# A gated-delta chain in two parts: its recurrence beside the inverse of the next head, each part with its own stretch of the waits

## The chip, the cores and the metric

The kernel runs on one core of a Trainium2 chip. The core has a matrix engine (TensorE, "PE" in the profile, its weight loads "PEld"), a vector engine (VectorE, "DVE"), a scalar engine (ScalarE, "ACT"), a general engine (GpSimd, "POOL") and a queue engine (SyncE, "SP") that issues the DMAs here. Each engine works through its own list of instructions in order and waits for the others by semaphores. Matrix products land in PSUM, which has eight banks; everything else lies in SBUF. The metric is the device time of one execution in microseconds, lower is better.

## The reference

One decoder layer with two groups of heads that read the same normalised stream (2048 prompt rows, 16 meta rows, 8 samples of 4 rows; width 1024): four retention heads and four gated-delta heads of 128 columns, then an output projection, a normalisation and a SwiGLU feed-forward part. What matters here is the gated-delta head, computed in chunks of 128 rows:

```python
decay = jnp.exp(jnp.where(incl, G[..., :, None] - G[..., None, :], -jnp.inf))
lower = jnp.where(strict, kk * decay, 0.0) * beta[..., :, None]
a_mat = jnp.eye(C, dtype=q.dtype) + lower
sol = lax.linalg.triangular_solve(a_mat, rhs, left_side=True, lower=True, unit_diagonal=True)
w_v, w_k = sol[..., :D], sol[..., D:]
attn = jnp.einsum('bnhid,bnhjd->bnhij', q, k) * decay
...
def step(s, xs):
    wv, wk, at, qg, kt, cd = xs
    u = wv - jnp.einsum('bhcd,bhde->bhce', wk, s)
    o = jnp.einsum('bhcd,bhde->bhce', qg, s) + jnp.einsum('bhij,bhje->bhie', at, u)
    s = cd[..., None, None] * s + jnp.einsum('bhcd,bhce->bhde', kt, u)
    return s, o
...
o_g = (rms_norm(o_g) * gdn_norm_w.astype(f32)).reshape(bsz, L, W) * jax.nn.silu(gz.astype(f32))
```

So a head has two parts. The triangular system of each chunk depends on that chunk alone, so all chunks of a block are inverted together. The recurrence over the state `s` goes chunk by chunk, and a head's recurrence in one block follows its recurrence in the block before.

## The kernel before

The program is written out in full by Python. It has three stages: attention (both groups of heads), the output projection with its normalisation, and the feed-forward part. The change touches attention alone.

Attention runs over four blocks of 512 prompt rows, that is four chunks of 128; the first block also carries one short tile with the meta and sample rows, which has a chain of its own beside the main one (`side` in `gdn_chain`). In each block the eight heads follow each other in the order r0 g0 r1 g1 r2 g2 r3 g3, in the fourth block r0 g0 g1 r1 g2 g3 r2 r3, with r for retention and g for gated delta. Each head has two kinds of work.

The *projection* (`ret_proj`, `gdn_proj`) multiplies the block with the head's weights, in many matmuls into PSUM tiles `pj`: 128x256 for a retention head, 128x512 for a gated-delta head. Weights and activations are split in a high and a low part, three matmuls for each product. Both are generators that yield every few matmuls with the microseconds that these are reckoned to take: 20.5 us for a whole projection of a block without the short tile. The vector and scalar engines work on what a projection leaves: rotation for r, convolution and gates for g. The convolved q goes into tile `post0`, the gate into `zg`, two buffers each.

The *chain* (`ret_chain`, `gdn_chain` with `gdn_group`) is a long line of small steps, each on what the step before left, through PE and DVE or ACT in turn. It starts when the head's projection is over, and its steps are strewn among the matmuls of the projections that follow. These are the steps of a gated-delta chain by their lines in the profile:

- L878 decay exponents (from `mg`), L895 transposes of v, L892 and L900 the scaled keys `kp` and their transposes, L906 the product of the keys, L908 `LT`, its masked parts L917 (`Z`), L918 (`U`) on DVE and L920 (`Lm`) on POOL;
- L924 the first transpose, then six levels of the inverse: L930, then L932 on DVE, then L937 and L939, then two copies on ACT;
- L950 the residual, L951 and L953 on DVE; two refinements L958, each followed by L960 on DVE, which leaves `V`; L965 the attention matrix;
- the recurrence, for each of four chunks: L992 and L993 the products of the state with keys and queries, L995 `r` on DVE, L1000 its product with the inverse, L1001 `u` on ACT, L1009 with L1010 the state update `S_gdn`, L1011 with L1012 the output row;
- the output: a reciprocal root in about a dozen short DVE operations (L261 to L273), L1019 and L1021 the scaling, L1023 the transposes, L1027 the product with the gate into `Uf`, L1029 the store.

The chain is a generator too. After each step it yields a number out of `LAT`, the microseconds that its result is reckoned to take, and yields `None` between the inverse and the recurrence; before the change `gdn_chain` swallows that `None` and lets the rest of the short tile's chain go first there. `attn_block` calls `advance` at each yield of a projection:

```python
self.active[key] = [chain, 0.0]
...
c[1] -= us
while c[1] <= 0:
    w = next(c[0], None)
    ...
    c[1] += w * SLACK[key]
```

So one `r` and one `g` chain are active at a time, and a `g` chain waits 1.8 times the reckoned latency at each step. `start` first calls `finish`, which lets an unfinished chain run out with no projection in between.

The tile framework then puts the recorded instructions in an order for each engine: it moves an instruction ahead of another on its engine where its operands are reckoned to be there earlier and its buffer is free. Small products of the chain share three PSUM banks (`w`), the state products one (`sc`), the projections two (`pj`). `LT`, `mg`, `Uf`, `V0` and `V1` have one buffer each; `E`, `kT`, `vb` and `kp` have two. Before the change the output lies in the buffer of `V0`, and the gated output in that of `Uf`, both of which the next head's inverse writes.

Of the kernel before, what the change touches and what calls it, by code (L numbers as in the profile page):

```python
# [31 lines left out]
RMS_EPS = 1e-6  # L32
NBLK = 4
CPB = 4
SLACK = {"r": 1.0, "g": 1.8}
LN_AT = [(x, i) for x in ("r1", "g1", "r2", "g2") for i in (18, 26)]
LAT = [1.0, 0.7, 0.7, 0.7, 2.0, 0.7, 0.5, 1.2, 1.8, 0.9, 1.0, 1.0, 1.7, 1.0, 0.6, 0.5, 0.5]
LEVELS = (1, 2, 4, 8, 16, 32, 64)


# [196 lines left out]
class Builder:  # L237
# [599 lines left out]
    def gdn_chain(self, b, h, cvz, G, mixd):  # L837

        cv, zg, sk, kps = cvz
        tiles = self.tiles_of(b)  # L840
        t = 1 if b == 0 else 0
        main = self.gdn_group(b, h, cv, zg, sk, kps[-1], G, mixd, list(range(t, t + CPB)), tiles)
        side = self.gdn_group(b, h, cv, zg, sk, kps[0], G, mixd, [0], tiles) if b == 0 else iter(())
        for w in main:
            if w is None:
                yield from side
                continue
            yield w
            w = next(side, None)
            if w is not None:  # L850
                yield w
        if b == NBLK - 1:
            self.nc.sync.dma_start(out=self.O["gdn_p"][h], in_=self.S["gdn", h])

    def gdn_group(self, b, h, cv, zg, sk, kp, G, mixd, ts, tiles):
# [10 lines left out]
        big = lambda tag, bufs=1, dt=F32, n=None: mp.tile([128, m, n or (R if sp else 128)], dt, tag=pre + tag, name=tag, bufs=1 if sp else bufs)  # L866
# [103 lines left out]
        yield None  # L970
        S = self.S["gdn", h]
        ss = self.sm.tile([128, m], F32, tag="gss", name="gss")
        O = big("V0", n=128)
        orow = NS if sp else 128
        for i in range(m):
            c0 = col(i)
# [42 lines left out]
        nc.vector.tensor_tensor(out=rs, in0=rs, in1=cq[:orow], op=ALU.mult)  # L1019
        p = self.psc.tile([128, 4, 128], F32, tag="sc", name="sc")[:, :m, :orow]  # L1020
        nc.vector.tensor_tensor(out=O[:orow], in0=O[:orow], in1=rs.unsqueeze(2).broadcast_to([orow, m, 128]), op=ALU.mult)  # L1021
        for i in range(m):
            nc.tensor.transpose(p[:, i, :], O[:orow, i, :], self.ident[:orow, :orow])  # L1023
        c0 = col(0)
        mx = big("Uf")[:, :, :orow]
        z = zg[:, c0:c0 + m * orow].rearrange("p (a b) -> p a b", a=m)
        nc.vector.scalar_tensor_tensor(out=mx, in0=p, scalar=self.gwh, in1=z, op0=ALU.mult, op1=ALU.mult)  # L1027
        cm = c0 if sp or b else c0 - NMETA
# [35 lines left out]

    def advance(self, us):
        for key in list(self.active):
            c = self.active[key]
            c[1] -= us
            while c[1] <= 0:
                w = next(c[0], None)  # L1070
                if w is None:
                    del self.active[key]
                    break
                c[1] += w * SLACK[key]

    def start(self, key, chain):
        self.finish(key)
        self.active[key] = [chain, 0.0]

    def finish(self, key):  # L1080
        while key in self.active:
# [2 lines left out]
    def attn_block(self, b):  # L1084
        nc = self.nc
        mixd = self.mixd[b]
        tiles = self.tiles_of(b)
        n = len(tiles)
        xT = self.xp.tile([128, 2, 8, 560], F32R, tag="xT", name="xT")
        self.xT = xT[:, 0], xT[:, 1]  # L1090
        before = self.first_block() if b == 0 else self.turned(b)
        next(before)
        rt = self.gp.tile([128, 5, 192], F32, tag="rott", name="rott", bufs=1)
        self.rot = {ch: rt[:, t] for t, (rows, c0, ch) in enumerate(tiles)}
        if b == 0:
            nc.sync.dma_start(out=rt[:SP, 0], in_=self.I["rot"][0:SP, :])
        o = SP + 512 * b
        nc.sync.dma_start(out=rt[:, n - CPB:n], in_=self.I["rot"][o:o + 512, :].rearrange("(c p) n -> p c n", p=128))
        gates = self.gp.tile([128, 5, 8], F32, tag="gates", name="gates")[:, :n]
        if b == 0:  # L1100
            nc.vector.memset(gates, 0.0)
        G = {}
        gg = self.gdn_gates(b, gates, G)
        ln = self.phase_ln(b + 1) if b < NBLK - 1 else iter(())
        for x in self.order(b):
            h = int(x[1])
            got = []
            if x[0] == "r":
                self.finish("r")
                fill = self.ret_proj(b, h, gates, got, before if h == 0 else None)  # L1110
            else:
                fill = self.gdn_proj(b, h, G, got)
            for i, us in enumerate(fill):
                self.advance(us)
                self.age += 1
                if self.pend and self.age >= 3 and self.age % 2:
                    self.split(*self.pend.pop(0))
                if x == "g0" and i == 8:
                    next(gg, None)
                if (x, i) in LN_AT:  # L1120
                    next(ln, None)
            if x == "r0":
                next(gg)
            if x[0] == "r":
                self.start("r", self.ret_chain(b, h, got, mixd))
            else:
                self.start("g", self.gdn_chain(b, h, got, G, mixd))
        for _ in ln:
            pass

# [329 lines left out]
```

## Time and profile before

| | |
|---|---|
| median of three runs | 3085.02 us (3084.47 to 3089.49) |
| profiled execution: time, span | 3085.82 us, 3084.0 us |
| mean granted TensorE clock | 0.972 |
| instructions in the span | 47091 |
| DMA | 384.75 MB, 125 GB/s mean |

The profile gives busy time by engine, busy time in stretches of the span, who waited for whom, and the instructions in order of time. PE's busy time overlaps from one matmul to the next, since matmuls are pipelined: what a matmul costs the engine is read from one start to the next. The projections can be told from the chains by name: `pj<-wh,xT` and `pj<-wl,xT` belong to a retention head, `pj<-xT,wh` and `pj<-xT,wl` to a gated-delta head. In a row of the waits stand the instruction that waited, what ended the wait, the total, the number of waits and the longest.

### The profile page before, as it was taken

The numbers are of one execution on the slowest core, as the hardware profiler recorded it, in microseconds if no ns is written. First come the engines' busy times: TensorE is split into PE (matmuls) and PEld (weight loads), VectorE is DVE, ScalarE is ACT, GpSimd is POOL, SyncE is SP. The second block draws the span as 40 slices with busy tenths as digits, with TensorE's granted clock in tenths as the row PEclk, the third lists the DMA queues.
The fourth block names the chain that finished last, engine by engine and source line by source line (L and its number), as shares of the span: only waits on it lengthen the run. The fifth ranks groups of instructions, "written<-read, shape, count | busy, mean of one in ns | idle before, by whom it ended". The sixth has DMA issues, their size and how long they took to land.

```text
span 3084.0 us, 47091 instructions
## 1 busy us (share of the span) xinstructions
PE 2889.0 (94%) x17930; PEld 2564.3 (83%) x17930; DVE 2189.5 (71%) x4547; ACT 1139.4 (37%) x2571; POOL 1055.6 (34%) x927
## 2 busy tenths in 40 slices
PE   6999998999999999999959999989999999999995
PEld 6888887888888877887848888889999988999994
DVE  7778676666676676567767777896666689666667
ACT  2444433444443433432233333433333343333331
POOL 1332222221222122225644545354334335333332
PEclk8999998999999999999979999989999999999998
DMA  7544533443344323346652222432212243221211
GB/s 268 211 158 175 178 141 132 155 156 145 130 153 169 116 91 122 117 151 208 206 175 97 95 85 89 144 122 76 75 55 76 73 130 130 75 76 55 76 62 41
DMA packets 132275, 384.75 MB, mean 125 GB/s; under 512 B 18145, under 2 KB 53521, under 8 KB 115665
## 3 DMA queue, kind: packets, MB, share of 16 engines
q1 hardware_dynamic: 132048, 381.74, 35.5%
q8 instruction: 141, 2.31, 0.3%
q14 instruction: 86, 0.70, 0.1%
HBM read 294.14 MB, written 87.56 MB: 124 GB/s over the span
## 4 chain that ended last, share of the span: by engine, by line
PE 58%; DVE 22%; POOL 7%; issue 7%; ACT 4%; DMA 3%; SPq 0%; POOLq 0%; ACTq 0%; DVEq 0%
PE pj L366 17%; PE d L366 15%; POOL S L1264 4%; PE Y L366 4%; PE X L366 4%; PE Z L366 4%; PE W L366 2%; DVE dl L316 2%; DVE s34l L316 1%; ACT s34h L309 1%; DVE rqt L267 1%; POOL Lm L920 1%; DVE cacc L820 1%; DVE y L1356 1%; DVE lnst L284 1%
## 5 line engine op out<-in xcount | busy, mean ns | idle before, releaser
L366 PE MATMUL pj<-wh,xT 128*128 128x256 f32 (+2 forms) x2176 | 453.4, 296 | 9.1 <-ACT wh L309 3.7
L366 PE MATMUL pj<-xT,wh 128*128 128x512 f32 (+1 forms) x1280 | 378.2, 379 | 0.8 <-DVE kp L775 0.6
L366 PEld LDWEIGHTS pj<-wh,xT 128*128 128x128 f32 (+1 forms) x2176 | 354.4, 191 | 14.1 <-ACT wh L309 4.0
L366 PE MATMUL pj<-wl,xT 128*128 128x256 f32 (+3 forms) x1088 | 315.3, 290 | 0.5 <-POOL wl L316 0.5
L366 PE MATMUL d<-dl,fh 128*128 128x512 f32 (+1 forms) x748 | 299.9, 401 | 8.4 <-DVE dl L316 7.8
L366 PE MATMUL d<-dh,fh 128*128 128x512 f32 (+1 forms) x748 | 293.8, 393 | 6.6 <-DVE y L1356 6.5
L366 PE MATMUL d<-dh,fl 128*128 128x512 f32 (+1 forms) x748 | 297.2, 397 | 0.7 <-POOL fl L316 0.7
L316 POOL TENSOR_TENSOR fl<-ta,fh 128x384 fp32r<-128x384 f32 (+1 forms) x66 | 70.8, 1073 | 642.5 <-ACT fh L309 642.5
L1264 POOL TENSOR_TENSOR S<-fr 128x512 f32<-128x512 f32 x132 | 209.7, 1606 | 168.1 <-DVE s34l L316 108.6
L1356 DVE TENSOR_TENSOR y<-y,d 128x512 f32<-128x512 f32 (+1 forms) x352 | 238.9, 680 | 31.7 <-PE d L366 31.6
L366 PE MATMUL pj<-xT,wl 128*128 128x512 f32 (+1 forms) x640 | 228.9, 358 | 0.0
L366 PEld LDWEIGHTS pj<-xT,wh 128*128 128x128 f32 x1280 | 207.4, 191 | 19.6 <-DVE S L674 3.0
L366 PEld LDWEIGHTS pj<-wl,xT 128*128 128x128 f32 (+1 forms) x1088 | 207.6, 191 | 1.1 <-POOL wl L316 0.8
L366 PEld LDWEIGHTS d<-dl,fh 128*128 128x128 f32 (+1 forms) x748 | 137.9, 184 | 39.9 <-DVE dl L316 21.8
L366 PEld LDWEIGHTS d<-dh,fl 128*128 128x128 f32 (+1 forms) x748 | 137.9, 184 | 33.9 <-POOL fl L316 1.1
L316 DVE TENSOR_TENSOR a11l<-fr,a11h 128x512 fp32r<-128x512 f32 x66 | 52.1, 789 | 160.2 <-ACT a11h L309 160.2
L366 PEld LDWEIGHTS d<-dh,fh 128*128 128x128 f32 (+1 forms) x748 | 138.1, 185 | 29.4 <-DVE y L1356 9.8
L920 POOL TENSOR_TENSOR Lm<-LT,lvl 128x512 f16<-128x512 f32 (+1 forms) x108 | 138.4, 1315 | 35.0 <-DVE LT L908 28.5
L309 ACT CAST a11h<-fr 128x512 fp32r<-128x512 f32 x66 | 41.0, 621 | 293.4 <-DMA fr<-gu 293.4
L366 PE MATMUL X<-b,a11h 128*128 128x384 f32 (+1 forms) x528 | 125.6, 322 | 19.2 <-ACT b L309 13.9
L531 POOL TENSOR_TENSOR qk<-qk,rotB 128x256 f32<-128x256 f32 (+1 forms) x68 | 51.3, 759 | 259.2 <-DVE rotB L530 202.0
L366 PE MATMUL Y<-t,s12h 128*128 128x384 f32 (+1 forms) x528 | 129.2, 330 | 7.0 <-ACT s12h L309 2.5
(333 smaller groups left out, 7904.3 us busy)
## 6 DMA issues: line engine op xcount, KB each, us to landing
fr<-gu SPq DMA_DIRECT2D x132, 512.0 KB, 3.9
wh<-parts SPq DMA_DIRECT2D x45, 1024.0 KB, 6.2
wl<-parts SPq DMA_DIRECT2D x45, 1024.0 KB, 6.8
fr<-dn SPq DMA_DIRECT2D x66, 512.0 KB, 3.9
parts<-wh SPq DMA_DIRECT2D x15, 1024.0 KB, 6.4
parts<-wl SPq DMA_DIRECT2D x15, 1024.0 KB, 7.5
raw<-wret SPq DMA_DIRECT2D x16, 512.0 KB, 7.0
raw<-wgd SPq DMA_DIRECT2D x16, 512.0 KB, 6.5
```

Source lines behind the costliest of these rows:

```text
L267: nc.vector.scalar_tensor_tensor(out=t, in0=y, scalar=a, in1=y, op0=ALU.mult, op1=ALU.mult)
L284: i = nc.vector.bn_stats(out=st[:, o], in_=x)
L309: i = nc.scalar.copy(out=h, in_=src)
L316: i = (nc.vector if el == "dve" else nc.gpsimd).tensor_tensor(out=l, in0=src, in1=h.bitcast(F32), op=ALU.subtract)
L366: self.nc.tensor.matmul(out, lhsT=a(k), rhs=b(k), start=first and k == 0 and i == 0, stop=last and k == kn - 1 and i == 2, skip_group_chec ...
L531: nc.gpsimd.tensor_tensor(out=o, in0=o, in1=B[:, :, ::-1, :], op=ALU.add)
L820: nc.vector.scalar_tensor_tensor(out=ac, in0=pre[:, i:i + N], scalar=w(i), in1=ac, op0=ALU.mult, op1=ALU.add)
L920: nc.gpsimd.tensor_tensor(out=Lm[:, x - 1], in0=LT, in1=lvl(x), op=ALU.mult)
L1264: op = lambda o, x, z, f: nc.gpsimd.tensor_tensor(out=o, in0=x, in1=z, op=f)
L1356: nc.vector.tensor_tensor(out=ys, in0=ys, in1=p, op=ALU.add)
```

## The change

The chain of a gated-delta head is cut at its `None`. At that point `advance` takes it out of the place `"g"`, runs out what is still in a new place `"h"`, and puts the rest of the chain there; so the inverse of the next head can start in `"g"` while the recurrence goes on in `"h"`. Each place has its own stretch. `pace` works it out: for the inverse, 0.9 times the projections up to the end of the next gated-delta projection, at `PROJ` = 25 us each, divided by the inverse's own waits (`INVERSE` = 21 us, twice that in the first block). That is 2.14 where a retention head lies between two gated-delta heads, 1.07 where none does and in the first block. The recurrence gets 3.0. For the last gated-delta head both parts get 1.64. Retention chains keep 1.0. The wait behind the step that writes `LT` grows from 0.9 to 1.8, and a new wait of 1.2 stands between the scaled output and its transposes. Since the old head's recurrence now runs while the next head writes `V0` and `Uf`, output and gated output get buffers of their own, `O` and `mxg`. No arithmetic is added or left out.

```diff
-SLACK = {"r": 1.0, "g": 1.8}
-LAT = [1.0, 0.7, 0.7, 0.7, 2.0, 0.7, 0.5, 1.2, 1.8, 0.9, 1.0, 1.0, 1.7, 1.0, 0.6, 0.5, 0.5]
+LAT = [1.0, 0.7, 0.7, 0.7, 2.0, 0.7, 0.5, 1.2, 1.8, 1.8, 1.0, 1.0, 1.7, 1.0, 0.6, 0.5, 0.5, 1.2]
+PROJ = 25.0
+INVERSE = 21.0
+REST = 8.0
...
             if w is None:
+                yield None
                 yield from side
...
-        O = big("V0", n=128)
+        O = big("O", n=128)
...
         nc.vector.tensor_tensor(out=O[:orow], in0=O[:orow], in1=rs.unsqueeze(2).broadcast_to([orow, m, 128]), op=ALU.mult)
+        yield LAT[17]
         for i in range(m):
             nc.tensor.transpose(p[:, i, :], O[:orow, i, :], self.ident[:orow, :orow])
...
-        mx = big("Uf")[:, :, :orow]
+        mx = big("mxg")[:, :, :orow]
...
     def advance(self, us):
         for key in list(self.active):
-            c = self.active[key]
+            c = self.active.get(key)
+            if c is None:
+                continue
             c[1] -= us
             while c[1] <= 0:
-                w = next(c[0], None)
-                if w is None:
+                w = next(c[0], self)
+                if w is self:
                     del self.active[key]
                     break
-                c[1] += w * SLACK[key]
-
-    def start(self, key, chain):
+                if w is None:
+                    del self.active[key]
+                    self.finish("h")
+                    self.active["h"] = [c[0], 0.0, c[3], 0.0]
+                    break
+                c[1] += w * c[2]
+
+    def pace(self, b, x):
+        seq = [(c, y) for c in range(NBLK) for y in self.order(c)]
+        i = seq.index((b, x))
+        nxt = [j for j in range(i + 1, len(seq)) if seq[j][1][0] == "g"]
+        inv = INVERSE * (2 if b == 0 else 1)
+        if not nxt:
+            f = 0.95 * PROJ * (len(seq) - 1 - i) / (inv + REST)
+            return f, f
+        return 0.9 * PROJ * (nxt[0] - i) / inv, 3.0
+
+    def start(self, key, chain, slack, later):
         self.finish(key)
-        self.active[key] = [chain, 0.0]
+        self.active[key] = [chain, 0.0, slack, later]
...
-                self.start("r", self.ret_chain(b, h, got, mixd))
+                self.start("r", self.ret_chain(b, h, got, mixd), 1.0, 1.0)
             else:
-                self.start("g", self.gdn_chain(b, h, got, G, mixd))
+                self.start("g", self.gdn_chain(b, h, got, G, mixd), *self.pace(b, x))
```

Three places show how the instructions move. The changed kernel's lines are 2 to 4 higher than those of before: L906 becomes L909, L908 L911, L918 L921, L924 L927, L958 L961, L992 L995, L1000 L1003, L1009 L1012, L1021 L1024, L1023 L1027, L1027 L1031.

The first is on DVE, in the third block beside r2's projection, where the product of g1's keys is turned into `LT` and `U` (L529, L530 and L592 belong to retention, and `V_10847` holds g0's output). Before:

```order
L272 SCALAR_TENSOR_TENSOR rqt<-rqt,rqa 128x4
L273 SCALAR_TENSOR_TENSOR rqy<-rqt,rqy 128x4
L1019 TENSOR_TENSOR rqy<-rqy,gsk 128x4
L592 TENSOR_SCALAR rkd<-qk,cb 128x128
L1021 TENSOR_TENSOR V_10847<-V_10847,rqy 128x512
L908 TENSOR_TENSOR LT<-w,mg 128x512
L1027 SCALAR_TENSOR_TENSOR Uf<-sc,gwh,zg 128x512
L917 TENSOR_TENSOR Z<-LT,lvl 128x512
L529 TENSOR_TENSOR qk<-pj,rott 128x256
L918 SCALAR_TENSOR_TENSOR U<-Z,ident 128x512
```

The same place in the changed kernel, where `S_gdn_254` is g0's state:

```order
L998 SCALAR_TENSOR_TENSOR r<-sc,ng,vb 128x128
L594 TENSOR_SCALAR rkd<-qk,cb 128x128
L531 TENSOR_TENSOR qk<-pj,rott 128x256
L532 TENSOR_TENSOR rotB<-pj,rott 128x256
L911 TENSOR_TENSOR LT<-w,mg 128x512
L920 TENSOR_TENSOR Z<-LT,lvl 128x512
L1013 SCALAR_TENSOR_TENSOR S_gdn_254<-S_gdn_254,eg,sc 128x128
L921 SCALAR_TENSOR_TENSOR U<-Z,ident 128x512
```

The scaling of g0's output and its product with the gate have left this place; g0 is in its recurrence here, and of it only one state update stands between `LT` and `U`.

The second is on PE, the two refinements of g0's inverse in the third block. Before, they stood among g1's projection:

```order
L958 MATMUL w<-mg,LT 128x128 x4
L366 MATMUL pj<-xT,wh 128x512 x2
L366 MATMUL pj<-xT,wl 128x512
L366 MATMUL pj<-xT,wh 128x512 x2
L366 MATMUL pj<-xT,wl 128x512
L366 MATMUL pj<-xT,wh 128x512 x2
L366 MATMUL pj<-xT,wl 128x512
L958 MATMUL w<-V_10809,LT 128x128 x4
```

Now they stand at the head of r2's projection, emitted without a wait between them because the next gated-delta head starts:

```order
L961 MATMUL w<-mg,LT 128x128 x4
L368 MATMUL pj<-wh,xT 128x256
L368 MATMUL pj<-wl,xT 128x256
L368 MATMUL pj<-wh,xT 128x256 x2
L368 MATMUL pj<-wl,xT 128x256
L368 MATMUL pj<-wh,xT 128x256 x2
L368 MATMUL pj<-wl,xT 128x256
L961 MATMUL w<-V_10912,LT 128x128 x4
```

Eight projection matmuls of 256 columns stand between the two where nine of 512 stood.

The third is on PE in the fourth block, where two gated-delta projections follow each other; `S_gdn_257` is the state of the third block's g3. Before, its last chunk lay in g0's projection, beside the first step of the next head:

```order
L366 MATMUL pj<-xT,wh 128x512
L992 MATMUL sc<-S_gdn_257,kT 128x128
L993 MATMUL w<-S_gdn_257,post 128x128
L878 MATMUL w<-mg,cb 128x128 x2
L1000 MATMUL sc<-r,V_13645 128x128
L878 MATMUL w<-mg,cb 128x128 x2
L1009 MATMUL sc<-u,kt 128x128
L1011 MATMUL w<-u,E 128x128
L895 MATMUL w<-ident,post 128x128 x4
```

Now it lies in g1's projection, among the levels of g0's inverse (L933 and L940):

```order
L933 LDWEIGHTS Lm
L933 MATMUL w<-T,Lm 128x128
L996 MATMUL w<-S_gdn_257,post 128x128
L1003 MATMUL sc<-r,V_13701 128x128
L1012 MATMUL sc<-u,kt 128x128
L940 LDWEIGHTS U
L940 MATMUL w<-Z,U 128x128
```

These rows are out of a run of three levels and the ends of the last two chunks in which no projection matmul stands.

## The prediction

> **What bounds it now.** First the page (busy time by engine, then the chain that ended last, by engine), then busy time by stage; its columns are the stretch, its length, then busy us of PE, PEld, DVE, ACT and POOL, the granted TensorE clock, the DMA share and GB/s.
>
> ```profile
> PE 2889.0 (94%) x17930; PEld 2564.3 (83%) x17930; DVE 2189.5 (71%) x4547; ACT 1139.4 (37%) x2571; POOL 1055.6 (34%) x927
> PE 58%; DVE 22%; POOL 7%; issue 7%; ACT 4%; DMA 3%; SPq 0%; POOLq 0%; ACTq 0%; DVEq 0%
> 13.00:1340.30 1327.30, 1246.83 (x9140) 1094.51 (x9141) 913.25 (x2530) 539.89 (x1599) 313.17 (x382) 0.97 0.41 151
> 1560.00:3084.00 1524.00, 1433.25 (x7796) 1301.93 (x7796) 1114.59 (x1675) 531.32 (x874) 624.56 (x456) 0.97 0.27 89
> ```
>
> TensorE carries the chain. The change touches only the attention stage, up to 1340.3 us; the output projection and the feed-forward part behind it (1560 to the end) start when attention ends and keep their length. In attention PE is idle for 1327.30 - 1246.83 = 80.5 us, and DVE, next busiest, fills 913.25 of 1327.30, 69%. So what can be won is at most about 80 us of waits, and the list of what PE waits for in this stretch (total us, times, longest) says which:
>
> ```profile
> PE sc L1023 <- DVE V L1021: 18.1, 15, 2.2
> PE w L924 <- DVE U L918: 14.0, 11, 2.9
> ...
> PE sc L1000 <- DVE r L995: 4.8, 14, 0.5
> ...
> PE w L937 <- DVE Z L932: 1.9, 3, 0.9
> ...
> PE sc L992 <- DVE S_gdn L1010: 1.3, 4, 0.3
> ...
> PE sc L1000 <- ACT qs L997: 1.1, 3, 0.8
> ...
> PE w L937 <- ACT U L944: 0.9, 2, 0.5
> ...
> PE sc L1009 <- ACT u L1001: 0.7, 2, 0.4
> ```
>
> These eight are waits of the gated-delta chain: 18.1 + 14.0 + 4.8 + 1.9 + 1.3 + 1.1 + 0.9 + 0.7 = 42.8 us in 54 waits. The other 38 us (start, normalisation, retention chains, weights) are not touched. The two large ones are one event. Third block, start of r2's projection, in order of time (start, us, engine, line):
>
> ```profile
> 880.65 1.05 PE L906 MATMUL w<-kT 128*128 128x128 f32 x8
> ...
> 881.79 0.72 DVE L273 SCALAR_TENSOR_TENSOR rqy<-rqt,rqy 128x4 f32<-128x4 f32 x1
> ...
> 882.82 0.69 DVE L1021 TENSOR_TENSOR V<-V,rqy 128x512 f32<-128x512 f32 x1
> 883.42 0.68 DVE L908 TENSOR_TENSOR LT<-w,mg 128x512 f32<-128x512 f32 x1
> 883.56 0.66 PE L1023 MATMUL sc<-ident,V 128*128 128x128 f32 x4 [1.86 <-DVE V L1021]
> ...
> 884.26 0.75 DVE L1027 SCALAR_TENSOR_TENSOR Uf<-sc,gwh,zg 128x512 f32<-128x512 f32 x1
> ...
> 884.93 0.97 DVE L917 TENSOR_TENSOR Z<-LT,lvl 128x512 f16<-128x512 f32 x1
> ...
> 885.94 0.28 PE L366 MATMUL pj<-wl,xT 128*128 128x256 f32 x1
> 886.05 0.39 PE L366 MATMUL pj<-wh,xT 128*128 128x256 f32 x2
> 886.16 1.33 DVE L918 SCALAR_TENSOR_TENSOR U<-Z,ident 128x512 f16<-128x512 f16 x1
> 886.29 0.28 PE L366 MATMUL pj<-wl,xT 128*128 128x256 f32 x1
> ...
> 887.54 0.40 PE L924 MATMUL w<-identh,U 128*128 128x128 f16 x4 [0.62 <-DVE U L918]
> ```
>
> PE stands 1.86 us at the old head's output transposes (L1023), because DVE is still in the normalisation (L273 to L1021). The new head's LT needs L906, over at 881.70, but starts at 883.42 behind that work, and L917 only behind L1027: so PE stands a second time at L924. Projection matmuls fill the rest: from 885.94 to 886.29 three of them, so 0.117 us each of 256 columns.
>
> **The change, part by part.**
>
> *The output transposes get a wait of their own, and the recurrence of the old head lies beside the inverse of the new.* Between the last L1011 and L1023 in this place the old order has 4.7 us of PE work (matmuls counted at 0.117 us and the like), the new 7.1. The wait was 1.86, the added cover 2.4: gone. In the third block's g3 and the fourth block's g1, g2 and g3 the new cover is 3.9 to 5.5, so there some of it stays.
>
> *LT no longer queues behind the output.* In the new order of DVE neither the output scaling nor the output product stands between LT and U; a state update does. From L906's end: 0.68 (L908) + 0.97 (L917) + 0.35 for an update (L1010, below) + 1.33 (L918) = 3.3 us. Between L906 and L924 PE now has 36 projection matmuls and five of the recurrence, 5.4 us at 0.117 and 0.23 each, where it had 22 (2.6 us) and the four transposes. Gone in 12 to 13 heads; the fourth block's g0 and g2 keep only 2.5 us of cover and may still wait 0.5 to 1 us each.
>
> *The links of the recurrence.* Where nothing queues, one chunk runs so:
>
> ```profile
> 1014.18 0.39 PE L992 MATMUL sc<-S_gdn,kT 128*128 128x128 f32 x2
> ...
> 1015.01 0.49 PE L1000 MATMUL sc<-r,V 128*128 128x128 f32 x2 [0.22 <-DVE r L995]
> 1015.86 0.49 PE L1009 MATMUL sc<-u,kt 128*128 128x128 f32 x2 [0.35 <-ACT u L1001]
> ...
> 1016.38 0.35 DVE L1010 SCALAR_TENSOR_TENSOR S_gdn<-S_gdn,eg,sc 128x128 f32<-128x128 f32 x1
> ```
>
> 0.83 us from L992 to L1000 and 0.85 to L1009, and before there was 0.4 to 0.7 us of other work between L1000 and L1009. With the stretch of 3.0 there are 0.7 to 2.3 us: most of 4.8 + 1.1 + 1.3 + 0.7 goes. The 1.9 + 0.9 of L937 is the end of the first block, where the old code emitted the rest of a chain at once; the new order has 2 us or more there.
>
> *What each wait takes beyond its idle time.*
>
> ```profile
> 634.54 1.11 PE L965 MATMUL w<-post,kT 128*128 128x128 f32 x8
> ...
> 635.48 0.39 PE L992 MATMUL sc<-S_gdn,kT 128*128 128x128 f32 x2
> ```
>
> L906's eight passes at 880.65 end at 881.70; but eight such passes behind which nothing waits (L965, two for each float32 matmul, so 0.23 each) take 0.94 us from start to start, not 1.05. That is 0.11 us per wait, 54 x 0.11 = 6 us. Together 42.8 + 6 = 48.8 us to be won.
>
> *What it adds.* (a) Between the two steps that refine the inverse the new order keeps 8 projection matmuls of 256 columns, 0.94 us, for nine of 512 before. Fourth block before, with a queue on DVE:
>
> ```profile
> 1311.72 0.63 PE L958 MATMUL w<-mg,LT 128*128 128x128 f32 x4
> ...
> 1313.14 0.68 DVE L960 TENSOR_TENSOR V<-Uf,w 128x512 fp32r<-128x512 f32 x1
> ...
> 1313.87 0.66 PE L958 MATMUL w<-V,LT 128*128 128x128 f32 x4 [0.39 <-DVE V L960]
> ```
>
> 2.15 us from step to step. Four matmuls of 0.11 and 0.94 make 1.4, so up to 0.75 us in each of 13 heads, 10 us in all; nothing where DVE is free. I take 4, nearer to free, since DVE is 69% busy and only its short operations queue there. (b) In the fourth block g0 is followed by g1 with no retention between. The recurrence of the head before them must end within one projection: 22.8 us reckoned (7.6 of waits x 3.0) against 20.5. q and the gate have two buffers, so g1's writes of them wait for that recurrence, and the new order has a run there of 3.7 us of PE work without one projection matmul. Two chunks in a row there take 2 x (0.83 + 0.85) and two updates, about 5 us; so 1 to 5 us lost in each of two places. I take 2.5 each, 5. (c) U in g0 and g2: 0 to 3 together, I take 1. (d) Leftovers of the covered waits, 0 to 8: I take 2. (e) The two new buffers, O and mxg, cost no instruction. The moved output store is one DMA on SP for each head as before; behind it on SP stand weight loads that are issued a projection ahead.
>
> **Sum.** 48.8 - 4 - 5 - 1 - 2 = 37 us. The profiled execution took 3085.82 us (span 3084.0 and 1.8 around it), 0.8 above the median 3085.02; from the median 3048.
>
> **Rivals.**
>
> *The new waits take half.* (a), (b), (c) and (d) at their upper ends, 10 + 10 + 3 + 8 = 31, leave 18: 3068. For it: every one of them follows from code order. Against: they would have to fall together. 0.15.
>
> *The clock rises too.* Attention is granted 0.97. If fewer stops bring back a third of the missing 3% of 1327 us, that is 13 us more: 3035. The rows of two stages with the same 509 matmuls speak against it:
>
> ```profile
> 794.40:867.50 73.10, 69.80 (x509) 61.50 (x509) 49.18 (x146) 30.04 (x88) 16.87 (x20) 0.98 0.37 138
> 867.50:940.60 73.10, 68.78 (x509) 59.93 (x509) 51.72 (x147) 30.68 (x89) 19.29 (x22) 1.00 0.41 152
> ```
>
> 0.98 and 1.00 took the same 73.10 us, so I count nothing for it. The Trainium skill, "TensorE: Matmul & The Clock Gate", Part 1, says that the array falls to half rate after an idle window of about 3.4 us; by that rule a denser stream would also run at a higher clock. These two rows do not show that it takes time here. 0.10.
>
> *Slower: a held PSUM bank.* The recurrence keeps one of three `w` banks from L993 until the output row of its chunk is read, and the new pace stretches that. If an inverse step then finds no free bank, PE, which runs in order, stands with all projection matmuls behind it. There are 4 x 16 = 64 chunks. From 37 / 64 = 0.58 us each the change loses; at 1 us each 64 us are paid: 3085 - 37 + 64 = 3112. Against: a step of the inverse needs at most two banks at once, and the order puts at most one pair of steps inside a chunk. 0.06.
>
> *It only moves the waits.* DVE runs in order too, and 51.72 of 73.10 us is busy; if U or V then queue behind projection work as long as before, the time stays at 3085, give or take 6. That includes that the change doesn't do what it says: its 25 us for a projection are 20.5 by the code's own count, so the inverse isn't over when the next head starts and its last steps are emitted at once. The new order shows that for the last two refinements alone. 0.07.
>
> **Numbers.** Forecast 3048 with 0.62 (3032 to 3062), and 0.15, 0.10, 0.07, 0.06 for the rivals in that order. Range 3024 to 3074: it holds the forecast, the first two rivals, and leaves out the last two and tails. About 0.2%, 6 us, is what a measurement of this kernel can tell from no change. Faster: 0.62 + 0.15 + 0.10 = 0.87; within 0.2% 0.07; slower 0.06.
>
> **What would show it.** In the profile after: the waits of the output transposes for the scaled output and of the first inverse product for U fall from 18.1 and 14.0 to under 5 together; the wait for r falls under 2; a pair of projections in the third block takes 68.5 to 70 us for 73.10; attention ends near 1303; the stretch behind it keeps its 1744 us. A wait of the second refinement above 8 us, or one of projection matmuls for the gate or for q in the fourth block above 10 us, would be the first rival; a wait of inverse matmuls that ends with the output row of a chunk, the third. It is wrong if attention shrinks but the tail behind it grows.

## The result, and the profile after

| | before | changed |
|---|---|---|
| time, median (range), us | 3084.74 (3084.2 to 3089.49) | 3042.91 (3039.83 to 3046.38) |
| ratio, 95% interval | | 0.9861 (0.9844 to 0.9878) |
| profiled execution (span), us | 3085.82 (3084.0) | 3041.72 (3039.9) |
| granted clock over the span | 0.972 | 0.977 |

The forecast was 3048 us, with a range of 3024 to 3074. The busy time by stage of the changed kernel (stretch, length, busy us of PE, PEld, DVE, ACT and POOL, granted clock, DMA share, GB/s):

```profile
12.50:1296.60 1284.10, 1226.03 (x9140) 1082.71 (x9141) 906.77 (x2530) 549.06 (x1599) 296.66 (x382) 0.98 0.43 157
1296.60:1519.00 222.40, 209.18 (x996) 168.37 (x994) 155.36 (x322) 65.51 (x95) 118.48 (x84) 0.98 0.63 199
1519.00:3039.90 1520.90, 1428.57 (x7789) 1298.03 (x7788) 1116.02 (x1675) 530.45 (x873) 621.83 (x454) 0.97 0.27 89
```

Attention ends at 1296.6 us, 43.7 earlier than before; the rest takes 222.40 + 1520.90 = 1743.3 us, as it did (1743.7). Of the gain, 22.4 us are idle time of TensorE (80.5 before, 1284.10 - 1226.03 = 58.1 now) and 20.8 us are busy time, for the same 9140 matmuls (the two stretches are counted from 13.0 and 12.5 us, hence 43.2 and not 43.7). The waits of TensorE in attention (total us, times, longest):

```profile
PE w L903 <- DVE kp L895: 13.9, 7, 2.6
...
PE w L940 <- DVE Z L935: 4.6, 4, 1.2
PE sc L1027 <- DVE O L1024: 4.4, 8, 1.1
...
PE w L961 <- DVE rqt L264: 1.9, 2, 1.0
PE w L961 <- DVE V L963: 1.8, 9, 0.3
PE w L961 <- DVE LT L956: 1.6, 2, 1.0
...
PE sc L1003 <- DVE r L998: 1.5, 1, 1.5
PE w L933 <- ACT T L946: 1.4, 4, 0.5
PE sc L1012 <- ACT u L1004: 1.3, 4, 0.4
PE w L927 <- DVE U L921: 1.3, 2, 0.6
```

Line numbers are 2 to 4 higher than before. The output transposes (L1027) wait 4.4 us where it was 18.1, the first inverse product (L927) 1.3 where it was 14.0, r 1.5 for 4.8. At the top stands a wait that the prediction has no term for: the key transposes of a new head (L903) wait 13.9 us for the scaled keys `kp`. Three pairs of projections of the third block (a retention head's and the gated-delta head's behind it), starting at r0, r1 and r2, show where:

```profile
708.40:777.20 68.80, 68.22 (x518) 60.85 (x516) 44.97 (x152) 32.45 (x97) 14.23 (x18) 1.00 0.36 132
777.20:845.70 68.50, 67.65 (x509) 59.77 (x508) 49.49 (x139) 30.43 (x87) 16.99 (x20) 1.00 0.40 147
845.70:918.90 73.20, 69.56 (x509) 61.25 (x509) 53.19 (x149) 31.67 (x88) 19.41 (x22) 0.98 0.40 152
```

The pair from r1 fell to 68.50 us (73.10 before); the one from r2 did not. In it, and in the pair from r3, the keys come late. Rows of r3's projection, all engines in order of time (start, us, engine, line):

```profile
924.65 0.16 DVE L274 SCALAR_TENSOR_TENSOR rqt<-rqt,rqa 128x8 f32<-128x8 f32 x1
...
924.81 2.50 POOL L306 TENSOR_TENSOR xa<-xa 128x512 f32<-128x512 f32 x2 [9.45 <-DMA wl<-parts]
925.32 0.79 DVE L275 SCALAR_TENSOR_TENSOR rqy<-rqt,rqy 128x8 f32<-128x8 f32 x1
...
926.63 0.70 DVE L273 TENSOR_TENSOR rqt<-rqy 128x8 f32<-128x8 f32 x1
...
927.26 0.41 DVE L531 TENSOR_TENSOR qk<-pj,rott 128x256 f32<-128x256 f32 x1
927.33 1.28 POOL L886 TENSOR_TENSOR mg<-E,cb 128x512 f32<-128x512 f32 x1
...
927.59 1.04 DVE L274 SCALAR_TENSOR_TENSOR rqt<-rqt,rqa 128x8 f32<-128x8 f32 x1
...
931.00 0.68 DVE L895 TENSOR_TENSOR kp<-kp,gsk 128x512 f32<-128x512 f32 x1
...
931.83 0.41 PE L903 MATMUL w<-ident,kp 128*128 128x128 f32 x2 [2.56 <-DVE kp L895]
```

`kp` needs an inverse square root, 12 operations on 128x8 values. One takes 0.16 us at 924.65 and 0.70 to 1.04 as soon as GpSimd (POOL) works beside it. GpSimd's L306 belongs to the normalisation of the next block's rows, whose steps are issued at 18 and 26 of the 32 steps of a projection, so the last lands where the next head begins. This led to theory P, which the prediction did not have: **a short VectorE operation beside GpSimd takes several times as long, and the waits are made of chains of such operations.** Each output normalisation is one too: 13 short operations and the scaling of the output, 3.3 us in all when nothing disturbs it.

### The profile page after: what moved, and what is told of

Read it like the earlier page. It is cut to its first block, busy times and chain, and to the rows that moved or that the text cites. A ratio compares the mean times of both kernels' runs of the same rounds, so it can differ in the third digit from the quotient of the medians.

```text
span 3039.9 us, 47059 instructions
## 1 busy us (share of the span) xinstructions
PE 2865.1 (94%) x17930; PEld 2550.1 (84%) x17930; DVE 2184.7 (72%) x4547; ACT 1148.7 (38%) x2571; POOL 1039.0 (34%) x927
## 4 chain that ended last, share of the span: by engine, by line
PE 59%; DVE 21%; issue 6%; POOL 6%; ACT 4%; DMA 3%; SPq 0%; POOLq 0%; ACTq 0%; DVEq 0%
PE pj L368 18%; PE d L368 16%; PE Y L368 4%; PE X L368 4%; POOL S L1288 4%; PE Z L368 4%; PE W L368 3%; DVE dl L318 2%; DVE s34l L318 1%; ACT s34h L311 1%; DMA fr<-bd 1%; DVE cacc L822 1%; ACT junk L773 1%; DVE y L1380 1%; DVE lnst L286 1%
## 5 line engine op out<-in xcount | busy, mean ns | idle before, releaser
L368 PE MATMUL X<-b,a11h 128*128 128x384 f32 (+1 forms) x528 | 125.5, 322 | 18.1 <-ACT b L311 13.9
L822 DVE SCALAR_TENSOR_TENSOR cacc<-cpre,cw,cacc 128x512 f32<-128x512 f32 (+1 forms) x144 | 115.8, 805 | 32.0 <-ACT cacc L820 30.5
L368 PE MATMUL Y<-t,s34h 128*128 128x384 f32 (+1 forms) x528 | 128.8, 328 | 8.5 <-DVE u L1325 4.3
L368 PEld LDWEIGHTS pj<-xT,wl 128*128 128x128 f32 x640 | 122.7, 192 | 16.8 <-issue 0.8
```

The source lines that it names most:

```text
L368: self.nc.tensor.matmul(out, lhsT=a(k), rhs=b(k), start=first and k == 0 and i == 0, stop=last and k == kn - 1 and i == 2, skip_group_chec ...
L822: nc.vector.scalar_tensor_tensor(out=ac, in0=pre[:, i:i + N], scalar=w(i), in1=ac, op0=ALU.mult, op1=ALU.add)
```

## The experiments

For each run the table counts, out of 520 operations of these square roots on 128x4 and 128x8 values in attention, those that lie for more than half of their time beside a GpSimd instruction (median length 0.16 us without, 0.72 us beside it in the kernel before). In that kernel 52 of the 520 take more than 0.4 us, and all 52 are among the 68 that lie beside GpSimd.

| run | us, median | ratio, 95% interval | beside GpSimd |
|---|---|---|---|
| before | 3084.74 | 1 | 68 |
| changed | 3042.91 | 0.9861 (0.9844 to 0.9878) | 38 |
| two_waits_alone | 3105.22 | 1.0055 (1.004 to 1.007) | 81 |
| cut_without_two_waits | 3089.36 | 1.0006 (0.9997 to 1.0015) | 69 |
| wait_behind_lt_back | 3070.35 | 0.9946 (0.9929 to 0.9963) | 61 |
| cut_old_stretch | 3127.76 | 1.0130 (1.0113 to 1.0147) | 107 |
| shared_buffers | 3045.84 | 0.9866 (0.9849 to 0.9882) | 38 |
| before_pool_free | 3034.34 | 0.9824 (0.9806 to 0.9841) | 35 |
| after_pool_free | 3013.50 | 0.9753 (0.9739 to 0.9768) | 20 |
| old_stretch_pool_free | 3033.22 | 0.9817 (0.9801 to 0.9834) | 41 |
| pool_added | 3080.51 | 0.9975 (0.9963 to 0.9988) | 68 |
| ln_earlier | 3018.79 | 0.9772 (0.9758 to 0.9787) | 21 |
| ln_all_earlier | 3018.50 | 0.9779 (0.9764 to 0.9794) | 14 |
| masks_on_vector | 3002.67 | 0.9727 (0.9713 to 0.9742) | 12 |

Time follows the last column closely among the kernels that do the whole work. That alone is a correlation; the runs that change GpSimd's work and nothing else test it.

**The parts of the change, one by one.** First the two waits without the cut:

```diff
-LAT = [..., 1.8, 0.9, 1.0, 1.0, 1.7, 1.0, 0.6, 0.5, 0.5]
+LAT = [..., 1.8, 1.8, 1.0, 1.0, 1.7, 1.0, 0.6, 0.5, 0.5, 1.2]
...
+        yield LAT[17]
         for i in range(m):
             nc.tensor.transpose(p[:, i, :], O[:orow, i, :], self.ident[:orow, :orow])
```

> The kernel before with the two waits alone (the one behind the step that writes LT 0.9 to 1.8, a new one of 1.2 ahead of the output transposes), no cut, old stretch 1.8. Theory A (the cut does it: the old chain is 47.7 us of stretched waits in 41 us of projections, so its end is always emitted at once, with the output scaling and the new head's LT next to each other on VectorE): the waits for V at the output transposes stay above 12 us (18.1 before), U falls a little (14.0 to 9 to 12); time 3075 to 3085. Rival B (the longer waits alone put the cover there): both waits fall under 8 together, time 3055 or less.

The waits for U fell to 9.5 us and those for V stayed large, as theory A said, but the kernel became slower, 1.0055, which neither theory said: the waits of the output transposes rose from 18.1 to 33.0 us in 13. The shifted steps put 7 of the 16 normalisations beside the level masks of GpSimd, where 3 lay before. Then the cut without the waits (`LAT[9]` at 0.9 and the `yield LAT[17]` taken out), and with only the wait behind LT back (`LAT[9]` at 0.9):

> The changed kernel with the wait behind LT back at 0.9 and none ahead of the output transposes; cut, both stretches and buffers stay. Theory A (the cut does it): most of the gain stays, 3043 to 3055; the waits for O at the output transposes rise from 4.4 us to 8 to 15 in 16 heads, those for U from 1.3 to 3 to 6. Rival B (the waits do it): 3065 or more, with U back near 14.

> The changed kernel with the wait behind LT alone back at 0.9; the wait of 1.2 ahead of the output transposes stays. Without both the changed kernel gained nothing (ratio 1.0006). Theory L (the wait ahead of the transposes covers the 3.3 us of a normalisation): most of the gain is back, ratio 0.986 to 0.992, waits for O under 8 us, those for U 4 to 9. Rival M (the wait behind LT moves the whole chain behind it to a place where fewer short operations lie beside GpSimd): ratio 0.995 or more, with 55 or more short operations beside GpSimd (38 in the changed kernel, 69 without both waits).

Without the two waits nothing is left of the gain (1.0006). The time is the one that rival B gave, the waits are not: 19.6 us for O, 18.2 for kp, and 8.2 for U, not near 14. With the wait ahead of the transposes, those for O fall to 2.1 us and for U to 6.0, as theory L said, but kp stays at 18.2 in 12 waits and the ratio, at 0.9946, lies nearer to theory M's than to L's. So the wait ahead of the transposes brings about 0.6% (1.0006 to 0.9946) and the one behind LT 0.85% (0.9946 to 0.9861); it shifts all that follows, and with it the meetings with GpSimd (61 to 38 in the table).

The cut with the old stretch of 1.8 for both parts:

```diff
-            return f, f
-        return 0.9 * PROJ * (nxt[0] - i) / inv, 3.0
+            return 1.8, 1.8
+        return 1.8, 1.8
```

> The changed kernel with 1.8 for both parts in place of what pace works out (2.14 or 1.07 for the inverse, 3.0 for the recurrence); the cut, the two waits and the buffers stay. Theory A1 (the cut alone, at any stretch): within 6 us of the changed kernel, 3037 to 3050. Rival A2 (the stretch of the recurrence makes the cover between r, u and S): the waits for r, u, S and qs of the recurrence return (7.9 us before in all, under 4 in the changed kernel), and with the inverse of the first and fourth block cut short (1.8 for 1.07, so the rest emitted at once) waits for Z, T and U of 10 us or more: 3055 to 3070.

Slower than any theory allowed: 1.0130, with 50.1 us of waits for O in 16 and 14.7 for S. The projection of r2 in the third block shows the reason (start, us, engine, line):

```profile
911.52 7.73 POOL L923 TENSOR_TENSOR Lm<-LT,lvl 128x512 f16<-128x512 f32 x6 [2.40 <-DVE LT L911]
...
915.95 1.09 DVE L264 TENSOR_SCALAR rqt<-rqa 128x4 int32<-128x4 int32 x1
917.08 1.09 DVE L265 TENSOR_SCALAR rqy<-rqt 128x4 int32<-128x4 int32 x1
918.21 1.07 DVE L273 TENSOR_TENSOR rqt<-rqy 128x4 f32<-128x4 f32 x1
919.22 0.71 POOL L533 TENSOR_TENSOR qk<-qk,rotB 128x256 f32<-128x256 f32 x1
919.31 0.65 DVE L274 SCALAR_TENSOR_TENSOR rqt<-rqt,rqa 128x4 f32<-128x4 f32 x1
919.99 0.16 DVE L275 SCALAR_TENSOR_TENSOR rqy<-rqt,rqy 128x4 f32<-128x4 f32 x1
...
922.52 0.69 DVE L1024 TENSOR_TENSOR O<-O,rqy 128x512 f32<-128x512 f32 x1
...
923.27 1.11 PE L1027 MATMUL sc<-ident,O 128*128 128x128 f32 x4 [4.94 <-DVE O L1024]
```

With this stretch the old head's normalisation falls right beside the new head's level masks (L923), in 13 of 16 heads. Until these end at 919.25 an operation takes 1.07 to 1.09 us, beside the GpSimd product that follows (L533, to 919.93) 0.65; the first without company takes 0.16. TensorE stands 4.94 us. In the changed kernel, outside the first block, none meets these masks, and none in any block meets the two mask products of E, beside which 15 of the 16 lay before: the normalisation takes 4.4 us in the mean of 16 heads, for 6.5 before and 6.7 here.

Last the buffers (`O` in `V0`, gated output in `Uf`, as before the change):

> The changed kernel without its two new buffers: output and gated output again in those of V0 and Uf. Theory S (outside the fourth block the recurrence ends well ahead of the next inverse's last level, so the buffers are free by then): ratio 0.984 to 0.989, as the changed kernel's 0.986. Rival T (where g0 and g1 follow each other the next inverse's Uf and V0 wait for the old output to be sent, with TensorE behind them): 3 us or more of new waits that end with the output row or its store in each of two places, ratio 0.989 or more.

0.9866, as theory S said: the two buffers are worth nothing that can be measured here.

**GpSimd's work alone.** In three kernels the two mask products of E and the level masks were left out, with TensorE's order untouched (in the third, 10 of 14,048 rows stand otherwise):

```diff
-        Es = mg
+        Es = E
...
-        nc.gpsimd.tensor_tensor(out=Es, in0=E, in1=bc(ST), op=ALU.mult)
-        nc.gpsimd.tensor_tensor(out=E, in0=E, in1=bc(M1), op=ALU.mult)
...
-        for x in range(1, nl):
-            nc.gpsimd.tensor_tensor(out=Lm[:, x - 1], in0=LT, in1=lvl(x), op=ALU.mult)
+        nc.scalar.activation(out=Lm[:, 0], in_=LT, func=AF.Copy, scale=0.01)
...
-                nc.tensor.matmul(py[:, i, :], lhsT=Lm[:, x - 1, i, :], rhs=T[:, i, :], start=True, stop=True)
+                nc.tensor.matmul(py[:, i, :], lhsT=Lm[:, 0, i, :], rhs=T[:, i, :], start=True, stop=True)
```

> The kernel before, leaving out what GpSimd does for the inverse: the two mask products of E and the masks of the levels above the first (one scaled copy of LT on ScalarE stands for all of them). TensorE's order is that of the kernel before, row by row. Theory P (a short VectorE operation takes 0.16 us alone and 0.7 to 1.2 beside GpSimd, and the waits come from the 13 of a normalisation): the normalisation of the outputs falls from a mean of 6.5 us to under 4.5, the waits for V at the output transposes from 18.1 to under 6, those for U from 14.0 to under 7, time 3045 to 3065. Rival Q (the order of VectorE's queue alone, as the prediction had it): the waits keep three quarters of their size and the time is 3078 or more.

> The changed kernel with the same work of GpSimd left out; TensorE's order is unchanged. Theory P: little is left to win, since few of its normalisations lie beside GpSimd (mean 4.3 us): 3025 to 3040, so that the distance to the kernel before with the same left out falls from 42 us to 30 or less, half of it to 20 the likeliest. Rival Q: the distance stays at 35 to 45.

> The cut with the old stretch of 1.8 (3128 us, 50.1 us of waits for O), with the same work of GpSimd left out; TensorE's order differs in 10 rows of 14,048. Theory P (there the normalisation of nearly every head fell beside the six level masks of the next): the waits for O fall from 50.1 to under 12, the normalisation from 6.7 to under 4.5 us, time 3065 or less. Rival Q (too little cover at 1.8, whatever GpSimd does): the waits for O stay above 25 and the time above 3095.

The stage of attention and the waits of TensorE in the kernel before, so cut:

```profile
13.00:1288.50 1275.50, 1230.68 (x9140) 1082.66 (x9140) 851.96 (x2529) 549.21 (x1618) 128.83 (x234) 0.98 0.43 157
```

```profile
PE sc L1023 <- DVE V L1021: 5.4, 10, 0.7
PE sc L1000 <- DVE r L995: 4.8, 14, 0.5
...
PE w L937 <- DVE Z L932: 1.8, 3, 0.9
...
PE sc L992 <- DVE S_gdn L1010: 1.3, 4, 0.3
PE sc L1000 <- ACT qs L997: 1.1, 3, 0.8
```

This separates the eight waits. The two large ones go, 18.1 to 5.4 and 14.0 to none that the list shows; the small links of the recurrence (r 4.8, S 1.3, qs 1.1) stay to the tenth. VectorE does the same work (2529 instructions for 2530) in 851.96 us for 913.25: 61 us of its busy time came from the company of these products. The product that makes U is part of it: beside its own head's level masks it takes 1.20 us in the mean of 16 heads, without them 0.68. In the changed kernel, so cut, the wait for kp falls from 13.9 us with the row normalisation left where it is:

```profile
PE w L903 <- DVE kp L895: 4.7, 7, 0.9
```

In the third kernel the waits for O fall from 50.1 us to:

```profile
PE sc L1027 <- DVE O L1024: 5.4, 14, 0.6
```

and 3127.76 us become 3033.22. Of the 85 us by which the old stretch is slower than the changed kernel, 19.7 are left without these products (3033.22 for 3013.50): most of the loss was the company, the rest goes with the stretch. All three times came out within or below theory P's, and theory Q is out for the two large waits; a detail missed is the normalisation in the kernel before, which fell to 4.9 us and not under 4.5. (A product left out also shortens what depends on it; the added products below have nobody that depends on them.) What is left between before and changed without this work is 3034.34 - 3013.50 = 20.8 us, half of the 42: the part of the change that doesn't hang on these products. It comes with the new stretches, since the cut at the old one is only 1.1 us below the kernel before when both lack these products (3033.22 for 3034.34); which of the stretches brings it no run separates. Now the opposite, four products that nobody needs at the end of each recurrence of the changed kernel:

```diff
+            if i == m - 1 and not sp:
+                spare = mp.tile([128, m, 128], F32, tag="spare", name="spare", bufs=1)
+                for j in range(4):
+                    nc.gpsimd.tensor_tensor(out=spare, in0=V, in1=u.unsqueeze(1).broadcast_to([128, m, 128]), op=ALU.mult)
             yield LAT[16]
```

> The changed kernel with four products of 128x512 added on GpSimd at the end of each recurrence, into a spare tile that nobody reads, so about 5 us of GpSimd beside the normalisation of each output; orders of TensorE and VectorE are unchanged. Theory P: the normalisation grows from 4.3 us to 7 or more, the waits for O at the output transposes from 4.4 to 25 to 50, time 3068 to 3095. Rival Q (GpSimd has 20 to 30% load in attention, its work is free): within 6 us of 3043.

The loss came as theory P said (0.9975 for 0.9861, some 35 us), but not where: the normalisation grew only to 6.0 us and the waits for O to 7.9, those for Z from 4.6 to 21.5 in 11. Third block, r2's projection:

```profile
904.53 5.38 POOL L1023 TENSOR_TENSOR spare<-V,u 128x512 f32<-128x512 f32 x4 [4.24 <-ACT u L1004]
...
905.87 1.33 DVE L269 SCALAR_TENSOR_TENSOR rqt<-rqy,rqa 128x1 f32<-128x1 f32 x1
907.23 0.16 DVE L270 SCALAR_TENSOR_TENSOR rqy<-rqt,rqy 128x1 f32<-128x1 f32 x1
907.42 1.15 DVE L299 SCALAR_TENSOR_TENSOR lnnm<-lnmv,rqy 128x1 f32<-128x1 f32 x1
...
909.88 1.23 DVE L304 TENSOR_TENSOR xa<-xa 128x1024 f32<-128x1024 f32 x1 [1.05 <-ACT xa L302]
...
911.28 0.68 DVE L935 SCALAR_TENSOR_TENSOR Z<-w,ident 128x512 f16<-128x512 f32 x1
...
912.02 0.38 PE L940 MATMUL w<-Z,U 128*128 128x128 f16 x4 [2.89 <-DVE Z L935]
```

The added products met the row normalisation's short operations (L269, L299), whose last step on VectorE (L304) came late by it, and Z stood behind that step in VectorE's queue; the output normalisation, from 912.53, came after the added products. The queue's order matters, here through operations that GpSimd stretches. The level masks were not late: TensorE's wait for them is 0.6 us here as in the changed kernel.

**The new wait, and a faster kernel.** The row normalisation moved away from the end of a gated-delta projection:

```diff
-LN_AT = [(x, i) for x in ("r1", "g1", "r2", "g2") for i in (18, 26)]
+LN_AT = [(x, i) for x in ("r1", "g1", "r2", "g2") for i in ((18, 26) if x[0] == "r" else (8, 16))]
```

> The changed kernel with the normalisation steps of the next block's rows that lie in a gated-delta projection moved from steps 18 and 26 of 32 to 8 and 16, away from the projection's end. Theory C (the new wait of the key transposes for kp, 13.9 us in 7, comes from the normalisation being in VectorE's queue when the new head's norms, scale and kp follow): the four waits of 2.6 us at the starts of the third and fourth retention projections go, that wait falls to 4 us or less, those four pairs of projections take 69 to 71 us for 73.2 to 77.8, and the time is 3027 to 3035. Rival D (kp is late because the old head's recurrence and the new inverse share VectorE whatever else runs): the waits stay above 9 us and the time within 4 us of 3043.

Ratio 0.9772, better than theory C's number. The move takes the row normalisation's VectorE operations away as well as GpSimd's L306, so this run alone can't tell theory C, VectorE's queue, from P; that the wait for kp fell to 4.7 us without GpSimd's mask products, the row normalisation in place, speaks for P. The waits, and the pairs from r1 and r2 of the third block, in this kernel:

```profile
PE w L903 <- DVE kp L895: 5.7, 4, 2.1
```

```profile
759.30:827.80 68.50, 67.62 (x510) 59.95 (x508) 51.85 (x147) 31.46 (x88) 20.23 (x22) 1.00 0.40 146
827.80:896.40 68.60, 67.64 (x509) 59.99 (x509) 51.94 (x147) 31.45 (x88) 20.40 (x23) 1.00 0.46 169
```

The pair from r2 now takes 68.60 us for 73.20, with the same work; what is left of the wait for kp lies in the first block. With the steps of the retention projections moved as well (10 and 18):

> As the run with the normalisation of the next rows at steps 8 and 16 of a gated-delta projection (ratio 0.977), and at 10 and 18 in place of 18 and 26 of a retention projection too. Theory P: in that run four output normalisations at the end of a retention projection (4.4 us for 3.3) still had 1.2 us of GpSimd's part of this step beside them; with it gone the waits for O fall from 4.4 to about 2 us and the time by 2 to 6: ratio 0.975 to 0.977. Rival: the earlier place meets the new head's inverse, whose Z and U then wait: Z above 8 us, ratio 0.979 or more.

No difference from the run before can be told (0.9779): the waits for O fell to 2.6 us, nearly as theory P said, those for Z rose to 9.3 as the rival said. And with the level masks made on VectorE one step ahead of their use:

```diff
-        for x in range(1, nl):
-            nc.gpsimd.tensor_tensor(out=Lm[:, x - 1], in0=LT, in1=lvl(x), op=ALU.mult)
...
+            nc.vector.tensor_tensor(out=Lm[:, x - 1], in0=LT, in1=lvl(x), op=ALU.mult)
             yield LAT[10]
```

> As ln_all_earlier, with the six masks of the levels made on VectorE, each one step ahead of its use, in place of GpSimd. VectorE gets about 64 main products of 0.7 us more per block of four heads (96 x 0.7 = 67 us in all), GpSimd loses as much and more. Theory P (GpSimd beside short operations is what costs): the two output normalisations of the first block fall from 8 and 9 us to under 5, the ratio is 0.970 to 0.977. Rival (VectorE's queue in order: every product in front of a Z or a U delays it): waits for Z above 15 us, ratio 0.980 or more.

Attention in ln_all_earlier, then in this kernel:

```profile
12.50:1276.20 1263.70, 1214.82 (x9139) 1076.98 (x9140) 902.25 (x2529) 545.50 (x1598) 298.58 (x382) 0.99 0.44 159
```

```profile
12.00:1260.50 1248.50, 1213.07 (x9140) 1077.43 (x9141) 909.17 (x2638) 546.23 (x1601) 183.15 (x274) 0.99 0.44 161
```

0.9727, and so 40 us less than the changed kernel. VectorE has 108 products more, 96 of them of 128x512 with a median of 0.68 us (six in each of 16 heads), and is busy for only 7 us more (909.17 for 902.25): what it takes over it saves in operations that GpSimd no longer stretches, the product that makes U, for one, with 0.68 us for 1.45 in the changed kernel. The rival's waits for Z did not come (0.3 us). The detail was wrong: the first two output normalisations of the first block took 13.0 and 9.6 us. There the rival's cause shows: of the 13 short operations only two in the first and one in the second are stretched (by L306 and L533), and most of the time other work of VectorE stands between them, level masks and products of 1.2 us.

## Why the prediction was right, and where it was not

**The bound and the tail** were right: TensorE's waits in attention, 43.7 us won there, the stretch behind it unchanged (1743.3 us).

**The two large waits** fell from 32.1 to 4.4 + 1.3 = 5.7 us, about as forecast (under 5). What failed is their cause. The prediction read the row "881.79 0.72 DVE L273" as VectorE being busy with the normalisation, and reckoned with cover and with what stands in front of LT in the queue. It did not ask why one operation of this chain took 0.72 us, and it put the stretched lengths of L917 and L918 (0.97 and 1.33 us, 0.69 and 0.68 without the mask products) into its sum as they stood. Without GpSimd's mask products, and with nothing moved, 26.7 of the 32.1 us go (before_pool_free). The wait for O falls in good part because the normalisation now lies mostly clear of the mask products; the same cut with another stretch put it onto them and lost 1.3%. The cover that the prediction reckoned with is real too: without the wait ahead of the transposes those for O are 19.6 us, though the normalisation is then hardly longer (4.7 us for 4.4). For U the cover does more: it still takes 1.45 us beside its own level masks, and its wait is 6.0 us with 0.9 behind LT and 1.3 with 1.8.

**The links of the recurrence** (7.9 us for r, S, qs and u) were forecast right, and for the right reason: in the kernel before they don't react to the mask products, and they fell to 3.4 us, r from 4.8 to 1.5. At the old stretch, without these products, r keeps 3.1 us and S takes 4.3.

**What it adds.** (a) The second refinement waits 1.8 us where I took 4; the first, which has no term, 1.9 + 1.6 at the same line. (b) The fourth block's squeeze: the waits for Z, T and u there, 2.3 + 1.4 + 1.3 = 5.0 us, for 5 (the other 2.3 for Z lie in the first block). (c) U 1.3 for 1. (e) Nothing, as said. But the sum lacks its largest term: 13.9 us for kp, 1.0 before. The first rival, "the new waits take half", did not name this wait; it says that the added waits would be those of (a) to (d).

**The clock.** I counted 6 us beyond the idle time and nothing for the clock; TensorE's busy time fell by 20.8. The trace's record of the clock has TensorE at half rate for 71.7 us of attention before and for 44.4 now, and busy for 62.5 and 41.7 us of these. Work at half rate takes about twice as long (three projection matmuls take 0.65 us from 661.60 in the kernel before, 0.35 at full rate), so by estimate (62.5 - 41.7) / 2 = 10 of the 20.8 us are this term; the rival to which I gave 0.10 happened in good part. My rows of 73.10 us at 0.98 and 1.00 were a weak test: the pair without loss of clock had more waits in it. No run held the clock fixed, so the split stays an estimate; what makes up the other 10 us, of which 6 were counted, is open. The Trainium skill ("TensorE: Matmul & The Clock Gate", Part 1) names an idle window of about 3.4 us as the condition; here less is enough, the last section shows half rate behind 1.85 us.

So it is luck that 3048 came so close to 3042.91: two errors cancel, a missing term of 13 us against a clock and pace term 15 us too small. **By place**, of the two pairs of 73.10 us for which I gave 68.5 to 70, the one from r1 came out at 68.50; the one from r2 stayed at 73.20 until the row normalisation was moved (68.60).

**The rivals.** A held PSUM bank: no wait of inverse matmuls ends with an output row. "Only moves the waits": true for kp alone. (From the median the first rival's sum gives 3085 - 18 = 3067, not 3068.)

## What to carry to other kernels

When an operation in a chain takes several times its usual length, look first at what the neighbouring engine does at that moment, before the queue's order; in a kernel like this one, where chains of tiny VectorE operations gate TensorE, placing them clear of GpSimd's large products can be worth as much as cover (here the two moves behind the changed kernel's 3043 us brought it to 3003). A change of spacing moves many such meetings at once, so test its parts together and apart: here each part alone was worth nothing or less, and the whole 1.4%. An engine with a low load is not free to use if its work slows a busier one.

## What the runs showed of the hardware

**VectorE beside GpSimd.** Operations of 0.16 us take up to 1.5 us beside GpSimd products in the kernel before, and up to 3.6 in pool_added. They end when GpSimd does: in the 14 kernels of the table 445 of the square roots' operations take more than 0.4 us, and each of the 445 ends 14 to 33 ns behind the end of a GpSimd instruction. Operations that read PSUM keep their length (L531 at 927.26 above, 0.41 us, and in the kernels before and changed 92 of this kind beside GpSimd, none over 0.43). One-input operations are hit on 128x4 and 128x8 (L264 above, 1.09 us) but not on 128x1: 147 of these lie beside GpSimd, none takes more than 0.16 us. The Trainium skill ("SBUF — State Buffer", "SBUF: two separate sides") says that VectorE and GpSimd share one pair of ports as an exclusive lock, held for a whole instruction, and that VectorE needs it for two SBUF inputs or a two-port mode. The traces agree as far as they go: the ends of the 445 are what waiting for a held lock would give. In which mode the one-input operations ran no trace shows.

**Half clock after short stops.** Two stretches of the kernel before, one behind the other:

```profile
658.00:661.40 3.40, 1.55 (x14) 1.36 (x13) 3.18 (x10) 0.00 (x0) 1.03 (x2) 1.00 0.01 2
661.50:664.90 3.40, 3.40 (x18) 3.40 (x18) 2.67 (x5) 0.00 (x0) 3.40 (x3) 0.50 0.20 77
```

TensorE was idle for 3.40 - 1.55 = 1.85 us of the first, in the wait for the output transposes, and the next 3.4 us were granted at half rate. By the rate above (0.65 us for 0.35) that costs about 1.5 us, an estimate: a stop of under 2 us can cost nearly its own length again, and removing it pays nearly twice. The clock record of this kernel changes in steps of 3.41 us. Of its 25 stretches at half rate 22 follow a step in which TensorE was idle for 1.83 us or more in all, in one stop or several; the other three follow 0.87 us or less. None of the 823 steps with full rate in them and behind them had more than 1.71 us. In the changed kernel the same two figures are 1.99 (14 of 16 stretches) and 1.97 us.
